# A hybrid block on one core: state-free products in one go, VectorE order anchored to matmuls, unscaled attention probabilities and tanh gates

## The chip, the cores and the metric

The kernel runs on one core of a Trainium2 chip. A core has five engines that work in parallel, each through its own instructions in order: TensorE (PE, matmuls and transposes; its weight loads are shown as PEld), VectorE (DVE), ScalarE (ACT), GpSimd (POOL) and SyncE (SP), which only issues DMAs. DMAs can also be issued from the queues of ACT and POOL. The metric is the device time of one execution in microseconds (us), the median over runs.

## The reference

One block of a network on 1024 tokens of width 1024, in fp32. An input norm is followed by a projection into three groups: q, k, v and a forget gate for 8 attention heads of 64; r, k, v and small low-rank paths for 8 recurrent heads of 64 (RWKV-7); and 2 x 1024 gate columns. Attention adds the running sum of the log forget gate to the logits, is causal, and ends in a softmax:

```python
logits = einsum('bhqd,bhkd->bhqk', q[:, :, q0:q1], k[:, :, :q1]) * scale
logits = logits + cum[:, :, q0:q1, None] - cum[:, :, None, :q1]
probs = softmax(where(causal, logits, -inf))
outs.append(einsum('bhqk,bhkd->bhqd', probs, v[:, :, :q1]))
```

The recurrence carries a 64x64 state per head over the tokens:

```python
sa = einsum('bhvk,bhk->bhv', state, a_t)
state = state * w_t[:, :, None, :] + sa[..., None] * b_t[:, :, None, :] + v_t[..., None] * k_t[:, :, None, :]
y_t = einsum('bhvk,bhk->bhv', state, r_t)
```

Both outputs are projected, multiplied by sigmoid of their gate columns, added and projected again (`wo`). A second norm, a gated feed-forward part of width 2816 with a convolution of three tokens, and a last norm end the block.

## The kernel before

Large products are done to nearly fp32 accuracy by splitting each operand into a rounded part and a remainder (`hi` and `lo`, written by a cast and a subtraction) and adding three matmuls. The stages in time are: the front (modulation, first norm) to 148 us; the recurrence, woven with the projections, to 655; attention, woven with the late gates, to 870; the branch projections `br` to 957, `wo` to 1056; the feed-forward up part (X, W, Y) to 1485 and its down part (D) to the end.

PE's order is written out by hand, by `Weave`. It keeps a clock `now`, advanced by a cost for each matmul emitted. Chains (generators) yield the time after which they want to go on; between them `fill` emits *filler* matmuls from a queue of projections (`qk`, `ps_rkv`, `v`, `gt`, later `rk_ps`). In the recurrence only PE is ordered so; a scheduler orders DVE, ACT, POOL and SP by itself. In attention DVE and ACT follow the written order too.

*Recurrence.* Eight units (4 head pairs `p` times 2 halves `hf` of the tokens) each have 8 chunks of 64 tokens. `pre` makes a unit's operands: the scan `cum` (L741), the vectors `ar`, `bk` and others on DVE, the products `p` masked into E (L789), which go through DRAM (`sm`) to the layout M; DVE inverts M in 31 steps of two operations (L809, L811), and the result E32 goes through DRAM (`se`) into TT (L814 to L823). `main` runs behind it, for the unit before: two transposes X<-TT on DVE (L866), then the products xi, zi, uw, mz, and the loop over chunks. For each chunk `fixed` emits the state-free products, two matmuls into `sp` and two into `yp`; two matmuls with the state S0 add to `sp`; DVE makes the next state S by a scaling (L929); two more matmuls with S0 add to `yp`; then 1.15 us of filler.

*Attention.* For each head `load_head` loads q and k (stA 128 rows, stB 68 rows) and v (vh) from POOL's queue. `s_chain` makes the logits `lg` of one block of 128 queries, `softmax` takes the maximum (L1075, DVE), the exp with its sum (L1079, ACT), the reciprocal (L1084) and scales P by it (L1085, DVE). `t_chain` transposes P on PE into `tp`, `halve` splits it (th on ACT, L1112; tl on DVE, L1115), `a_chain` multiplies with v into `ov`, and `collect` adds the two halves of `ov` into `o` (L1146 ACT, L1148 DVE); POOL splits a finished `o` into fx (L1155, L1156). Between these, `late_gate` emits 14 gate halves into the single PSUM tile `rk_ps`; `gate_out` evacuates one by five ACT operations (L1179 to L1187) and an addition on DVE (L1185) and stores it to d_gate. The weights of the late gates are split on POOL (L255, L259). Norms take ln and exp of a sum of squares (L287, L288 in `rms_rstd`); the norm behind `wo` is done in two halves of the tokens. ACT's functions come in sets, and a change of set is a row ACT_TABLE_LOAD; `use_ln_exp` (L195 to L199) asks for the set that has both ln and exp, at the start, after the sigmoids and ahead of the last norm.

Of the kernel before, what the change touches and what calls it, by code (L numbers as in the profile page):

```python
# [16 lines left out]
S = 1024  # L17
# [30 lines left out]
class Weave:  # L48
# [67 lines left out]
    def run(self, chains):  # L116

        self.live = [[self.now, 1 + i, g] for i, g in enumerate(chains)]
        while self.live:
            due = min((c for c in self.live if c[0] <= self.now), key=lambda c: (c[1], c[0]), default=None)  # L120
            if due is None:
                self.fill(min(c[0] for c in self.live))
                continue
            wait = next(due[2], None)
            if wait is None:
                self.live.remove(due)
            else:
                due[0] = self.now + max(wait, 0.0)
# [3 lines left out]
def hybrid_block(ctx: ExitStack, tc: tile.TileContext, a, out):  # L132
# [4 lines left out]
    def mm(o, lhsT, rhs, start, stop, more=False):  # L137

        weave.mm_cost(o, lhsT, rhs)
        nc.tensor.matmul(o, lhsT, rhs, start=start, stop=stop, skip_group_check=more)  # L140
# [34 lines left out]
    epsr = cp.tile([128, 3], F32, name="epsr")  # L175
# [28 lines left out]
    d_v = dr.tile([8, 128, 8, 128], F32R, name="d_v")  # L204
    d_orw = dr.tile([4, 128, S], F32, name="d_orw")
# [39 lines left out]
    def load_w(src, name, pool=None, n=1024, scale=None, tags=("whi", "wlo"), bufs=2):  # L245
# [7 lines left out]
        lo = pool.tile([128, n], F32R, tag=tags[1], name=f"lo_{name}", bufs=bufs)  # L253
        if weave.late == 1:
            i = nc.gpsimd.tensor_copy(hi, raw)  # L255
            if "head" in marks:
                tc.add_manual_dep(i.ins, marks["head"].ins.name, NOSYNC)
            for c in range(0, n, 256):
                nc.gpsimd.tensor_tensor(lo[:, c : c + 256], raw[:, c : c + 256], f32(hi[:, c : c + 256]), op=ALU.subtract)  # L259
        else:  # L260
            nc.scalar.copy(hi, raw)  # L261
            for c in range(0, n, NH):
                nc.vector.tensor_tensor(lo[:, c : c + NH], raw[:, c : c + NH], f32(hi[:, c : c + NH]), op=ALU.subtract)  # L263
# [71 lines left out]
    with ExitStack() as es:  # L335
# [388 lines left out]

        def pre(k, p, hf):
# [15 lines left out]
            nc.vector.tensor_tensor_scan(cum, C("reset"), cum, initial=0.0, op0=ALU.mult, op1=ALU.add)  # L741
            el = chunk_tile("el", 1, NCU, CH + 1)
            nc.gpsimd.memset(el[:, :, 0:1], 1.0)
            nc.scalar.activation(el[:, :, 1:], c3(cum), AF.Exp, scale=-DEC)
            en = tmp("en")
            nc.scalar.activation(en, cum, AF.Exp, scale=DEC)
# [5 lines left out]
            yield from head_sums(ssq, ksq, parts[:, 0, :], parts[:, 1, :])  # L752
            rn = tmp("ksq")
# [48 lines left out]
            ready = weave.now + (46000 if k == 0 else 38500)  # L802
            E32 = chunk_tile("E32", 1, 8, 32)
            nc.gpsimd.tensor_copy(E32, C("einit").rearrange("p (j t) -> p j t", t=32))
            t32 = tmp("t32", 256)
            for s in range(31):
                J, W = s // 4 + 1, 31 - s
                tv = t32[:, 0 : J * W].rearrange("p (j w) -> p j w", w=W)
                tt(tv, E32[:, 0:J, s : s + 1].to_broadcast([128, J, W]),  # L809
                   M32[:, s : s + 1, s + 1 : 32].to_broadcast([128, J, W]), op=ALU.mult)  # L810
                tt(E32[:, 0:J, s + 1 : 32], E32[:, 0:J, s + 1 : 32], tv, op=ALU.add)  # L811
            se = scr.tile([2, NCU, 2, 32, 32], F32, tag="se", name=f"se{n}")
            for g in range(4):
                nc.sync.dma_start(  # L814
                    se.rearrange("h c b (j g) t -> (h c b) g j t", g=4)[:, g, :, :],
                    E32[g * 32 : g * 32 + 32, :, :])
# [1178 lines left out]
```

## Time and profile before

| | us |
|---|---|
| median of 3 runs (lowest, highest) | 1701.3 (1697.85, 1704.96) |
| profiled execution: its time; span from first to last instruction | 1704.73; 1703.0 |
| recurrence, 148 to 655: PE busy, DVE busy, ACT busy | 489.3, 340.4, 216.2 of 507 |
| attention, 655 to 870: PE busy, DVE busy, ACT busy, POOL busy | 202.5, 165.5, 141.8, 52.4 of 215 |
| rest, 870 to 1485: PE busy | 614.9 of 615 |

A row of the profile names the line, the engine, the operation and its output and inputs by the program's names; "x4" counts equal instructions in a row, and brackets give idle time before it and what ended it. PE has the smallest idle time in every stage, and the table gives where it has any.

### The profile page before, as it was taken

Reading aid. Unit: us, or ns where it says so; the run is one execution under the profiler, and the core shown is the slowest. Engines: PE = TensorE matmul, PEld = TensorE weight load, DVE = VectorE, ACT = ScalarE, POOL = GpSimd, SP = SyncE. Lnnn points to the kernel's source line nnn. Section 1 sums busy time; section 2 is a strip of 40 time slices with the busy share of each in tenths; the row PEclk is TensorE's granted clock in tenths of the full one; section 3 lists DMA queues with packets and bytes.
Section 4 is the critical chain, followed back from the end, with each engine's and each line's share of the span. In section 5 each row is a group of like instructions: output and inputs, shape, how many; then the busy total and the mean of one; then the engine's idle time right before and its main releaser. Section 6 shows DMA issues by size and latency. Waiting matters only on the chain.

```text
span 1703.0 us, 26042 instructions
## 1 busy us (share of the span) xinstructions
PE 1638.0 (96%) x9772; PEld 1342.0 (79%) x9772; DVE 1220.8 (72%) x2390; ACT 808.6 (47%) x1482; POOL 143.4 (8%) x175
## 2 busy tenths in 40 slices
PE   5899999998999998999999999999999999999998
PEld 4767777786877776988878888888888888888886
DVE  5776787778676633888877634897777777787677
ACT  5453334333444554766642323654444444454455
POOL 0010101110111003123112000000000000000000
PEclk8899999999999999999999999999999999999999
DMA  8487743533342326433277611132333233484463
GB/s 328 139 314 205 192 125 97 136 106 106 91 115 75 91 81 151 141 110 107 76 265 268 246 62 63 50 105 94 123 107 103 93 117 101 163 284 153 125 215 112
DMA packets 120974, 239.85 MB, mean 141 GB/s; under 512 B 39888, under 2 KB 48336, under 8 KB 120848
## 3 DMA queue, kind: packets, MB, share of 16 engines
q1 hardware_dynamic: 112896, 220.94, 40.0%
q0 software_dynamic: 7952, 17.25, 3.8%
q8 instruction: 77, 1.26, 0.3%
q14 instruction: 49, 0.40, 0.1%
HBM read 172.59 MB, written 65.54 MB: 140 GB/s over the span
## 4 chain that ended last, share of the span: by engine, by line
PE 79%; DVE 9%; DMA 6%; ACT 2%; issue 2%; SPq 1%; DVEq 0%; ACTq 0%
PE X L140 13%; PE D L140 12%; PE Y L140 6%; PE wo L140 5%; PE br L140 5%; PE gt L140 5%; PE rk_ps L140 4%; PE qk L140 4%; PE ps_rkv L140 4%; PE W L140 3%; PE lg L140 2%; PE v L140 2%; PE ov L140 2%; PE sp L140 2%; PE tp L144 2%
## 5 line engine op out<-in xcount | busy, mean ns | idle before, releaser
L140 PE MATMUL D<-op,op 128*128 128x512 f32 x924 | 209.8, 390 | 0.0
L140 PEld LDWEIGHTS D<-op,op 128*128 128x128 f32 x924 | 173.5, 188 | 36.2 <-DVE op L1258 0.3
L140 PE MATMUL X<-T_m,S 128*128 128x512 f32 x440 | 107.3, 390 | 0.2
L140 PEld LDWEIGHTS X<-T_m,S 128*128 128x128 f32 x440 | 82.5, 188 | 18.2 <-ACT x L1534 0.6
L1257 ACT CAST op<-g 128x512 fp32r<-128x512 f32 x77 | 47.8, 621 | 74.1 <-PE D L140 48.0
L1258 DVE TENSOR_TENSOR op<-g,op 128x512 fp32r<-128x512 f32 x77 | 53.0, 689 | 41.7 <-ACT op L1257 41.7
L1494 DVE SCALAR_TENSOR_TENSOR c<-ab,vec,c 128x512 f32<-128x512 f32 x88 | 65.9, 750 | 19.5 <-ACT c L1497 17.9
L809 DVE TENSOR_TENSOR t<-E,M 128x60 f32<-128x60 f32 (+24 forms) x248 | 57.9, 233 | 30.2 <-DMA M<-sm 24.9
L1458 DVE TENSOR_TENSOR S<-ur,S 128x512 fp32r<-128x512 f32 x66 | 45.5, 691 | 35.6 <-ACT S L1454 35.5
L263 DVE TENSOR_TENSOR lo_in<-raw_in,hi_in 128x512 fp32r<-128x512 f32 x84 | 56.5, 707 | 16.1 <-PE gt L140 13.9
L1454 ACT CAST S<-ur 128x512 fp32r<-128x512 f32 x66 | 41.0, 622 | 55.6 <-DVE ur L1447 30.6
L1458 DVE TENSOR_TENSOR A<-ur,A 128x512 fp32r<-128x512 f32 x64 | 44.1, 688 | 30.9 <-ACT A L1454 30.7
L261 ACT CAST hi_in<-raw_in 128x1024 fp32r<-128x1024 f32 x42 | 44.0, 1049 | 44.3 <-PE ps_rkv L140 16.0
L140 PE MATMUL Y<-T_h,A 128*128 128x512 f32 x264 | 63.5, 390 | 0.0
L140 PE MATMUL Y<-T_h,S 128*128 128x512 f32 x264 | 63.3, 390 | 0.0
L140 PE MATMUL X<-B_b,A 128*128 128x512 f32 x252 | 60.8, 391 | 0.0
L140 PE MATMUL W<-B_f,A 128*128 128x512 f32 x252 | 60.6, 390 | 0.0
L1079 ACT ACTIVATE P<-lg,nm 128x896 f32<-128x896 f32 (+3 forms) x64 | 47.4, 743 | 22.8 <-DVE nm L1075 22.6
L811 DVE TENSOR_TENSOR E<-E,t 128x60 f32<-128x60 f32 (+24 forms) x248 | 53.8, 217 | 5.8
L140 PEld LDWEIGHTS Y<-T_h,A 128*128 128x128 f32 x264 | 49.6, 188 | 10.3
L140 PEld LDWEIGHTS Y<-T_h,S 128*128 128x128 f32 x264 | 49.6, 188 | 10.3
L1454 ACT CAST A<-ur 128x512 fp32r<-128x512 f32 x64 | 39.9, 623 | 34.2 <-PE X L140 31.5
(473 smaller groups left out, 4169.0 us busy)
## 6 DMA issues: line engine op xcount, KB each, us to landing
raw_in<-in_w_in SPq DMA_DIRECT2D x50, 512.0 KB, 3.7
wm<-in_w_mod SPq DMA_DIRECT2D x48, 512.0 KB, 7.0
ur<-in_w_up SPq DMA_DIRECT2D x44, 512.0 KB, 4.2
g<-d_g SPq DMA_DIRECT2D x35, 512.0 KB, 4.0
d_g<-gs SPq DMA_DIRECT2D x44, 256.0 KB, 2.0
d_g<-c SPq DMA_DIRECT2D x33, 256.0 KB, 4.4
d_st<-qh SPq DMA_DIRECT2D x64, 128.0 KB, 2.5
d_gate<-gs SPq DMA_DIRECT2D x32, 256.0 KB, 2.9
```

The lines of the kernel that those rows point to most:

```text
L140: nc.tensor.matmul(o, lhsT, rhs, start=start, stop=stop, skip_group_check=more)
L144: nc.tensor.transpose(o, i, eye)
L261: nc.scalar.copy(hi, raw)
L263: nc.vector.tensor_tensor(lo[:, c : c + NH], raw[:, c : c + NH], f32(hi[:, c : c + NH]), op=ALU.subtract)
L809: tt(tv, E32[:, 0:J, s : s + 1].to_broadcast([128, J, W]), M32[:, s : s + 1, s + 1 : 32].to_broadcast([128, J, W]), op=ALU.mult)
L811: tt(E32[:, 0:J, s + 1 : 32], E32[:, 0:J, s + 1 : 32], tv, op=ALU.add)
L1079: nc.scalar.activation(e[:, 0:n], lg[:, 0:n], AF.Exp, bias=nm[:, 0:1], accum_out=nm[:, 1:2])
L1257: nc.scalar.copy(hi, src)
L1258: tt(lo, src, f32(hi), op=ALU.subtract)
L1454: nc.scalar.copy(hi, src)
L1458: tt(lo, src, f32(hi), op=ALU.subtract)
L1494: stt(c, ab[:, x + hf * NH : x + hf * NH + NH], V("conv_w", 22 * x + i), c, op0=ALU.mult, op1=ALU.add)
```

## The change

*Recurrence.* The state-free products of all eight chunks are emitted in one go ahead of the chunk loop. Three DVE operations are *anchored*: a dependency without a wait puts them in the scheduler's order behind the matmul emitted last. These are the scan (now behind the ssq product), the first step of the inversion (spawned 8.5 us of the clock behind the `p` products) and the X transposes (1.5 us ahead of xi). `Weave.run` holds back the chain of `pre` when a step of `main` is due within 2.6 us.

*Attention.* For heads 0 to 6 P isn't scaled. The sums of four query blocks are collected, inverted by one reciprocal, transposed by PE (four rows), copied by ACT, stored to DRAM (d_rs) and loaded back, broadcast over 64 rows; both DMAs are issued from ACT's queue, and the load waits for the store. POOL multiplies the finished `o` with it. Head 7 goes as before. The first head is loaded by five DMAs of its own (`load_first`), so that the two buffers of `load_head` are both free for heads 1 and 2. A late gate is one tanh and one scaling with an offset; its weights are split on ACT and DVE. The table of exp and tanh is loaded by a preload of its own, and the one of ln and exp is asked for again after attention.

```diff
@@ Weave @@
-    def run(self, chains):
+    def run(self, chains, beside=0.0):
...
+        led = False
         while self.live:
             due = min((c for c in self.live if c[0] <= self.now), key=lambda c: (c[1], c[0]), default=None)
-            if due is None:
-                self.fill(min(c[0] for c in self.live))
+            lead = min((c[0] for c in self.live if c[1] < 2), default=None)
+            if due is None or (due[1] > 1 and not led and lead is not None and lead < self.now + beside):
+                self.fill(min(c[0] for c in self.live) if due is None else lead)
+                led = False
                 continue
+            led = beside > 0 and (led or due[1] < 2)
...
-        nc.tensor.matmul(o, lhsT, rhs, start=start, stop=stop, skip_group_check=more)
+        weave.last = nc.tensor.matmul(o, lhsT, rhs, start=start, stop=stop, skip_group_check=more)
+
+    def behind(i):
+        tc.add_manual_dep(i.ins, weave.last.ins.name, NOSYNC)
...
@@ load_w @@
+        nc.scalar.copy(hi, raw)
         if weave.late == 1:
-            i = nc.gpsimd.tensor_copy(hi, raw)
...
-            for c in range(0, n, 256):
-                nc.gpsimd.tensor_tensor(lo[:, c : c + 256], raw[:, c : c + 256], f32(hi[:, c : c + 256]), op=ALU.subtract)
-        else:
-            nc.scalar.copy(hi, raw)
-            for c in range(0, n, NH):
-                nc.vector.tensor_tensor(lo[:, c : c + NH], raw[:, c : c + NH], f32(hi[:, c : c + NH]), op=ALU.subtract)
+            weave.use("ACT", weave.now, 900)
+            weave.use("DVE", weave.now, 1200)
+        for c in range(0, n, NH):
+            nc.vector.tensor_tensor(lo[:, c : c + NH], raw[:, c : c + NH], f32(hi[:, c : c + NH]), op=ALU.subtract)
...
@@ the recurrence: inverse() holds lines 804 to 823 of before @@
+        def inverse(n, M32, TT, chunk_tile, tmp):
...
+                i = tt(tv, E32[:, 0:J, s : s + 1].to_broadcast([128, J, W]),
+                   M32[:, s : s + 1, s + 1 : 32].to_broadcast([128, J, W]), op=ALU.mult)
+                if s == 0:
+                    behind(i)
...
@@ pre @@
-            nc.vector.tensor_tensor_scan(cum, C("reset"), cum, initial=0.0, op0=ALU.mult, op1=ALU.add)
...
             yield from head_sums(ssq, ksq, parts[:, 0, :], parts[:, 1, :])
+            behind(nc.vector.tensor_tensor_scan(cum, C("reset"), cum, initial=0.0, op0=ALU.mult, op1=ALU.add))
...
-            ready = weave.now + (46000 if k == 0 else 38500)
...
+            ready = weave.now + (47500 if k == 0 else 38500)
             TT = chunk_tile("TT", 2, NCU, CH)
+            weave.spawn(inverse(n, M32, TT, chunk_tile, tmp), 8500)
...
@@ main @@
+            yield max(0, o["ready"] - weave.now - 1500)
             for h in range(2):
-                nc.vector.transpose(X[B0[h], :, :], TT[B0[h], :, 0:32])
-            yield max(0, o["ready"] - weave.now)
+                behind(nc.vector.transpose(X[B0[h], :, :], TT[B0[h], :, 0:32]))
+            yield 1500
...
-            def fixed(c):
-
+            for c in range(NCU):
                 alone = hf == 0 and c == 0
...
-            fixed(0)
             yield 2400
...
                     yield 1150
-                    fixed(c + 1)
...
-        weave.run([main_chain(), pre_chain()])
+        weave.run([main_chain(), pre_chain()], beside=2600.0)
@@ attention @@
+    def load_first():
+
+        parts = [d_st[0, 0], d_st[0, 1], d_st[0, 2, 0:68, :], d_st[0, 3, 0:68, :], d_v[0].rearrange("p a x -> p (a x)")]
+        tiles = [fxp.tile([128, S], F32R, tag=f"h{t}", name=f"first{t}") for t in (3, 7, 2, 6, 5)]
+        for t, x in zip(tiles, parts):
+            marks["head"] = nc.gpsimd.dma_start(t[0 : x.shape[0], :], x)
+        heads[0] = *tiles[0:4], tiles[4].rearrange("p (a x) -> p a x", x=128)
...
-    load_head(0)
+    load_first()
...
-            yield 10500
+            yield 3500
...
-            nc.scalar.activation(e[:, 0:n], lg[:, 0:n], AF.Exp, bias=nm[:, 0:1], accum_out=nm[:, 1:2])
+            p, hf = h // 2, i // 4
+            if (h, hf) not in sums:
+                sums[h, hf] = at.tile([128, 8], F32, tag="sums", name=f"sums{h}_{hf}", bufs=4), []
+            sm, done = sums[h, hf]
+            total = nm[:, 1:2] if h == 7 else sm[:, i % 4 : i % 4 + 1]
+            nc.scalar.activation(e[:, 0:n], lg[:, 0:n], AF.Exp, bias=nm[:, 0:1], accum_out=total)
...
-            nc.vector.reciprocal(nm[:, 2:3], nm[:, 1:2])
-            ts(e[:, 0:n], e[:, 0:n], nm[:, 2:3], None, op0=ALU.mult)
+            if h == 7:
...
+                ts(e[:, 0:n], e[:, 0:n], nm[:, 2:3], None, op0=ALU.mult)
...
+            if h < 7 and len(done) == 4:
+                yield t + 140 - weave.now
+                nc.vector.reciprocal(sm[:, 4:8], sm[:, 0:4])
+                inverse[h, hf] = weave.use("DVE", weave.now, 160) + 210, sm
+
+        def spread(h, hf, tp):
+            p = h // 2
+            rt = at.tile([4, 128], F32, tag="rt", name=f"rt{h}_{hf}", bufs=1)
+            nc.scalar.copy(rt, tp[0:4, 384:512])
+            t = weave.use("ACT", weave.now, 200)
+            nc.scalar.dma_start(d_rs[h, hf * NH : hf * NH + NH].rearrange("(i k) -> i k", k=128), rt)
...
+            yield t + 3500 - weave.now
+            nc.scalar.dma_start(norms[p, hf][h % 2 * 64 : h % 2 * 64 + 64, :],
+                                d_rs[h : h + 1, hf * NH : hf * NH + NH].to_broadcast([64, NH]))
+            landed.add((h, hf))
...
+                    last = jj == I and I in (1, 2) and h < 7
+                    if last:
...
+                        transpose(tp[0:4, 384:512], sm[:, 4:8], ident)
...
+            n = len(got)
+            if n == (2 if p == 3 else 4):
+                while (6 if p == 3 else h, hf) not in landed:
+                    yield 100
+                r = slice(0, 64 if p == 3 else 128)
+                for x in (slice(0, 256), slice(256, NH)):
+                    nc.gpsimd.tensor_tensor(o[r, x], o[r, x], norms[p, hf][r, x], op=ALU.mult)
...
-            nc.scalar.activation(g, rk_ps, AF.Abs)
-            nc.scalar.activation(m, rk_ps, AF.Relu, scale=-1.0)
-            weave.hold = weave.use("ACT", weave.now, 960) + 210
-            nc.scalar.activation(g, g, AF.Exp, scale=-1.0)
-            nc.scalar.activation(g, g, AF.Ln, bias=1.0)
...
-            tt(g, g, m, op=ALU.add)
...
-            nc.scalar.activation(g, g, AF.Exp, scale=-1.0)
+            nc.scalar.activation(g, rk_ps, AF.Tanh, scale=0.5)
+            weave.hold = weave.use("ACT", weave.now, 480) + 210
+            nc.scalar.activation(g, g, AF.Identity, scale=0.5, bias=epsr[:, 3:4])
...
+        nc.scalar.preload_act_table_set("exp_and_others")
         weave.run([a_chain(), t_chain(), s_chain()])
         weave.late = 2
         weave.run([drain()])
+    use_ln_exp()
```

Three places in the order. First DVE in the recurrence, where unit (1,1) runs its chunks (S1_1x is the state behind chunk x, made for the matmuls `sp` of the next chunk) while unit (2,0) waits for its transposes X2_0. Before:

```order
L929 TENSOR_SCALAR S1_11_4305<-sp1_1_4237,pcd1_1_2866 128x64
L763 SCALAR_TENSOR_TENSOR kr2_1_4247<-kr2_1_4247,vec_72,al2_1_4159 128x512
L866 STREAM_TRANSPOSE X2_0_4698<-TT2_0_3868 32x256
L764 TENSOR_TENSOR bk2_1_4249<-kr2_1_4247,en2_1_4165 128x8x64
L767 TENSOR_SCALAR al2_1_4159<-al2_1_4159,vec_72,oka_88 128x512
L866 STREAM_TRANSPOSE X2_0_4698<-TT2_0_3868 32x256
L929 TENSOR_SCALAR S1_12_4321<-sp1_1_4237,pcd1_1_2866 128x64
L768 TENSOR_TENSOR al2_1_4159<-al2_1_4159,k21_3355 128x512
L769 TENSOR_TENSOR bk2_1_4249<-al2_1_4159,en2_1_4165 128x8x64
L773 SCALAR_TENSOR_TENSOR ksq2_1_4261<-r21_3354,vec_72,al2_1_4159 128x512
L929 TENSOR_SCALAR S1_13_4337<-sp1_1_4237,pcd1_1_2866 128x64
```

and now:

```order
L939 TENSOR_SCALAR S1_16_4412<-sp1_1_4233,pcd1_1_2913 128x64
L821 TENSOR_TENSOR E2_1_4429<-p1_2_100_4432,cst2_122 128x4x128
L821 TENSOR_TENSOR E2_1_4429<-p1_2_110_4433,cst2_122 128x4x128
L268 TENSOR_TENSOR lo_v11_4379<-raw_v11_4376,hi_v11_4378 128x512 x2
L363 SCALAR_TENSOR_TENSOR v30_4071<-ps_rkv110_4384,omu_81,sh_rkv110_4453 128x512
L359 COPY sh_rkv31_5562<-pv3r_4314 128x1
L957 SCALAR_TENSOR_TENSOR y1_1_4426<-mu1_1_4428,y1_1_4426 128x512
L821 TENSOR_TENSOR E2_1_4429<-p1_2_104_4493,cst2_122 128x4x128
L821 TENSOR_TENSOR E2_1_4429<-p1_2_114_4494,cst2_122 128x4x128
L990 TENSOR_TENSOR vs1_0_4507<-v1_0_4465,vs1_0_4507 128x4x64
L848 COPY QA2_1_4430<-at2_1_4548 64x4x64 x4
L879 STREAM_TRANSPOSE X2_0_4603<-TT2_0_3839 32x256 x2
```

The transposes of the next unit stood between the second and the third state of a unit; now they stand behind its last state and its first normalisation step (y1_1).

Second, ACT in attention, about the end of head 0 (P is an exp, th a copy of transposed P, o an evacuation of `ov`, gs a gate, rt the sums, R their broadcast). Before:

```order
L1079 ACTIVATE P1_6_7207,nm1_6_7169<-lg1_6_7155,nm1_6_7169 128x896
L1112 CAST th0_22_7229<-tp0_22_7223 128x384
L1079 ACTIVATE P1_7_7242,nm1_7_7219<-lg1_7_7199,nm1_7_7219 128x1024
L1112 CAST th0_10_7265<-tp0_10_7256 128x512
L1146 COPY o01_7146<-ov_6889 64x256
L1112 CAST th0_11_7279<-tp0_11_7267 128x384
L1179 ACTIVATE gs10_1_7281<-rk_ps_6890 128x512
L1180 ACTIVATE gm10_1_7282<-rk_ps_6890 128x512
L1182 ACTIVATE gs10_1_7281<-gs10_1_7281 128x512
L1183 ACTIVATE gs10_1_7281<-gs10_1_7281 128x512
L1079 ACTIVATE P1_0_7308,nm1_0_7297<-lg1_0_7273,nm1_0_7297 128x128
```

and now:

```order
L1100 ACTIVATE P1_6_7146,sums1_1_7147<-lg1_6_7110,nm1_6_7127 128x896
L1119 COPY rt0_1_7149<-tp0_22_7118 4x128
L1121 DMA d_rs_97<-rt0_1_7149 4x128
L1195 COPY o01_7079<-ov_6895 64x256
L1100 ACTIVATE P1_7_7180,sums1_1_7147<-lg1_7_7138,nm1_7_7164 128x1024
L1159 CAST th0_10_7187<-tp0_10_7174 128x512
L1236 ACTIVATE gs9_1_7190<-rk_ps_6896 128x512
L1238 ACTIVATE gs9_1_7190<-gs9_1_7190,epsr_76 128x512
L1159 CAST th0_11_7198<-tp0_11_7182 128x384
L1100 ACTIVATE P1_0_7213,sums1_0_7214<-lg1_0_7194,nm1_0_7203 128x128
L263 CAST hi_in37_7220<-raw_in37_7218 128x1024
L1125 DMA R01_7152<-d_rs_97 64x512
```

The gate has two operations instead of five, the cast hi_in has come from POOL, and the store d_rs and the load R are issued with eight operations between them.

Third, ACT at the second half of the norm behind `wo` (the squares of the last rows, then ln and exp of the sums ssq2). Before:

```order
L1393 ACTIVATE wo6_0_10599,ssq2_10020<-h_sb6_10315 128x512
L1393 ACTIVATE wo6_1_10603,ssq2_10020<-h_sb6_10315 128x512
L1393 ACTIVATE wo7_0_10658,ssq2_10020<-h_sb7_10317 128x512
L1393 ACTIVATE wo7_1_10662,ssq2_10020<-h_sb7_10317 128x512
L287 ACTIVATE ssq2_10020<-ssq2_10020,epsr_76 128x4
L288 ACTIVATE ssq2_10020<-ssq2_10020 128x4
```

and now:

```order
L1448 ACTIVATE wo6_0_10543,ssq2_9964<-h_sb6_10259 128x512
L1448 ACTIVATE wo6_1_10547,ssq2_9964<-h_sb6_10259 128x512
L1448 ACTIVATE wo7_0_10602,ssq2_9964<-h_sb7_10261 128x512
L1448 ACTIVATE wo7_1_10606,ssq2_9964<-h_sb7_10261 128x512
L292 ACT_TABLE_LOAD
L292 ACTIVATE ssq2_9964<-ssq2_9964,epsr_76 128x4
L293 ACT_TABLE_LOAD
L293 ACTIVATE ssq2_9964<-ssq2_9964 128x4
```

Ln and exp each have a table load of their own; the preload written after attention stands at the start of ACT's order, in row 2.

112 lines of the change are left out of this document (61 added, 51 removed).

## The prediction

> **What bounds the kernel now.** I read the page's head and its chain of work first, then the busy time by stage.
>
> ```profile
> PE 1638.0 (96%) x9772; PEld 1342.0 (79%) x9772; DVE 1220.8 (72%) x2390; ACT 808.6 (47%) x1482; POOL 143.4 (8%) x175
> ...
> PE 79%; DVE 9%; DMA 6%; ACT 2%; issue 2%; SPq 1%; DVEq 0%; ACTq 0%
> ```
>
> ```profile
> 148.00:655.00 507.00, 489.29 (x4362) 390.23 (x4361) 340.44 (x968) 216.22 (x378) 58.92 (x83) 0.99 0.41 114
> 655.00:870.00 215.00, 202.46 (x1215) 176.48 (x1214) 165.48 (x324) 141.79 (x320) 52.42 (x64) 0.97 0.42 117
> ```
>
> TensorE is the bound: 96% of the span, and 79% of the chain that ended last. No matmul product is taken out by the change, so it can gain only where PE stands still. The second view (columns: window, its length, then busy us and count of PE, PEld, DVE, ACT, POOL, then clock) has the two stages that the change touches: the recurrence (148 to 655), where PE is idle for 507.00 - 489.29 = 17.7 us, and the attention (655 to 870), with 12.5 us. That is the whole prize, but for what a stall leaves behind. The waits of PE say whose these are, first in the recurrence, then in the attention (to 872):
>
> ```profile
> PE sp L140 <- DVE S L929: 8.6, 5, 3.5
> PE xi L140 <- DVE X L866: 3.0, 2, 1.6
> PE p L140 <- DVE bk L769: 2.0, 1, 2.0
> PE ps_rkv L140 <- DVE k L358: 1.6, 1, 1.6
> PE at L144 <- DVE E L789: 1.0, 1, 1.0
> ```
>
> ```profile
> PE rk_ps L140 <- ACT gm L1180: 4.7, 2, 4.5
> PE ov L140 <- DVE o L1148: 3.2, 2, 2.2
> PE br L140 <- ACT hi_br L1231: 2.1, 1, 2.1
> ```
>
> The largest of the recurrence is PE waiting for the state S. VectorE's timeline at one of its five waits shows why S is late, and PE's what follows:
>
> ```profile
> 421.72 0.43 DVE L866 STREAM_TRANSPOSE X<-TT 32x256 f32<-32x256 f32 x1 [3.80 <-DMA TT<-se]
> ...
> 423.68 0.28 DVE L929 TENSOR_SCALAR S<-sp,pcd 128x64 f32<-128x64 f32 x1
> ```
>
> ```profile
> 424.02 0.47 PE L140 MATMUL sp<-UV,E 128*64 128x64 f32 x4 [3.46 <-DVE S L929]
> ...
> 425.25 2.44 PE L140 MATMUL ps_rkv<-u_hi,lo_in 128*128 128x512 f32 x5
> ```
>
> S itself takes 0.28 us. It was queued behind an X transpose of the *next* unit, which waited 3.80 us for a DMA. And after the 3.46 us gap five matmuls take 2.44 us, where five take about 1.15 at the usual 0.23 each: a tail of 1.3 us. Of the five waits for S two are long (this one and one at 531 us), so the recurrence loses 17.7 + 2 x 1.3 = 20.3 us. In the attention, ScalarE and VectorE rows:
>
> ```profile
> 665.92 0.60 ACT L1179 ACTIVATE gs<-rk_ps 128x512 f32<-128x512 f32 x1 [5.46 <-DMA d_gate<-gs]
> ```
>
> ```profile
> 660.58 1.98 PE L140 MATMUL rk_ps<-u_hi,lo_in 128*128 128x512 f32 x8
> 667.06 3.78 PE L140 MATMUL rk_ps<-u_hi,hi_in 128*128 128x512 f32 x8 [4.51 <-ACT gm L1180]
> 670.64 3.22 PE L140 MATMUL rk_ps<-u_lo,hi_in 128*128 128x512 f32 x8
> ```
>
> ```profile
> 737.69 3.66 DVE L1085 TENSOR_SCALAR P<-P,nm 128x384 f32<-128x384 f32 x1
> ...
> 741.92 0.49 DVE L1085 TENSOR_SCALAR P<-P,nm 128x512 f32<-128x512 f32 x1
> ```
>
> ```profile
> 738.34 2.79 POOL L259 TENSOR_TENSOR lo_in<-raw_in,hi_in 128x256 fp32r<-128x256 f32 x4
> ```
>
> A gate evacuation waited for the store of an earlier gate (4.51 us on PE, then a tail of (3.78 - 1.98) + (3.22 - 1.98) = 3.0). A scaling of P took 3.66 us where a larger one takes 0.49, and it spans the whole of GpSimd's four subtractions; the `ov` matmul behind it waited 2.2, with a tail that I estimate at 2.3 (between the 1.3 and 3.0 above). So the attention loses 12.5 + 5.3 = 17.8 us.
>
> **The change, part by part.** *Recurrence order.* In the changed order the X transposes of a unit stand behind the last S of the unit before (the order shown above), the scan behind the ssq product, the inversion 8.5 us of PE's time later. Summed over the recurrence, VectorE's longest waits are
>
> ```profile
> DVE S L929 <- PE sp L140: 27.4, 24, 2.8
> DVE t L809 <- DMA M<-sm: 24.9, 7, 6.7
> DVE X L866 <- DMA TT<-se: 23.3, 12, 4.9
> ```
>
> The last two, those of the inversion and of the X transposes, are 48 us of head-of-line blocking. Of this, and of the scan's wait for its input, PE felt 8.6 (sp), 1.6 (ps_rkv, k behind the scan) and 1.0 (at). These 11.2 and the tails of 2.6 go: 13.8. The waits of unit 0 stay (xi 3.0, p 2.0), since nothing runs before it that its order could be put behind. But the anchors are no free good: with the products in one go a step of the state loop loses 0.38 us of PE work that used to lie between S and its use:
>
> ```profile
> 629.74 0.34 PE L140 MATMUL sp<-UV,E 128*64 128x64 f32 x4
> ...
> 630.12 0.33 PE L140 MATMUL sp<-S,Mt 64*64 64x64 f32 x4
> ```
>
> From 629.74 to 630.12 are the state-free products of a chunk, behind them those with the state. VectorE's rows between two S are unchanged in sum, so about ten of the sixty steps, those with over 2.2 us of VectorE rows between them by the changed order, now make PE wait. Bounds: 0 and the whole 0.38 in each of sixty steps, 23; I take 0.4 in ten, 4 us, as most steps hold under 2 us of such rows. The products themselves are the same matmuls; batching them saves between 0 and 0.1 for each of 56 groups (their starts are already close), I take 2. Recurrence: 13.8 - 4 + 2 = 12 us, bounds 0 and 25.
>
> *Attention.* Three of five gate operations, the lo_in subtractions on GpSimd and the P scaling of seven heads leave: 42 operations of ScalarE, 56 scalings and 14 additions of VectorE. Neither is the bound, so by themselves they are worth what PE waited for them: 4.5 + 3.0 (the first gate), 2.2 + 2.3 (the 3.66 us scaling, which can't recur without the GpSimd subtractions), 2.1 for hi_br (in the changed order 42 gate matmuls, moved and not removed, cover that end) and half of the remaining 3.7, so 16. New on PE: 14 transposes of four rows at about 0.11 (the 64-row groups above are 0.1 each), 1.5. New in front: the first head's logits come 35 matmuls (8 us at 0.23) behind the last `va`, where 54 stand before, and their second operands are 68-row loads, the third and fourth of five, with three heads loading at once instead of two. The 128-row load of 1 MB and, in the second row, the 68-row one of 544 KB take, from issue to landing:
>
> ```profile
> stA<-d_st POOLq DMA_DIRECT2D x7, 1024.0 KB, 5.9
> ```
>
> ```profile
> DMA to landing us min/median/max: 11.5/12.8/18.6
> ```
>
> In the changed kernel the latter comes in two halves, issued behind GpSimd's last operation of the recurrence and the 128-row loads, so about at the last `va`, 8 us before PE asks for them. In half of 11.5 they land in time, in the whole 12.8 they land 5 us late; I take 1.5. *The Trainium skill, "DMA: Bandwidth & Descriptors", section "Why a DMA increments its semaphore by 16 and not by 1", says that a transfer is spread over the largest number up to 16 that divides its rows, so 68 rows use 4 engines. The trace agrees in so far as this load, of half the bytes, takes twice as long as the 128-row one; by the rule two halves on separate engines would land in time, and this term would be 0.*
>
> *ScalarE's queue.* 14 times a store of the sums and a broadcasting load that waits for it are issued from ScalarE, with 5 to 9 operations (3 to 5 us at 0.6) between them; ScalarE is in order, so exp and the tp copies stand behind that wait. The nearest row is the gates' store:
>
> ```profile
> DMA to landing us min/median/max: 2.0/2.8/7.9
> ```
>
> At the median it costs nothing, at the longest 3 to 5 us each. I take three late by 0.5 us beyond PE's buffers, 1.5 us; bounds 0 and 14 x 4 = 56. Attention: 16 - 1.5 - 1.5 - 1.5 = 11.5, bounds 17 and a loss.
>
> *Table loads.* After attention the set with both ln and exp isn't reloaded in place (the load is hoisted to the start, so ScalarE's order shows), and each half of the norm behind `wo` gets two loads. Of the second half, ScalarE's exp, PE's rows and a load:
>
> ```profile
> 1061.10 0.21 ACT L288 ACTIVATE ssq<-ssq 128x4 f32<-128x4 f32 x1
> ```
>
> ```profile
> 1059.19 2.96 PE L140 MATMUL W<-B_f,A 128*128 128x512 f32 x12
> 1061.98 3.73 PE L140 MATMUL tr<-dg,h_sb 128*128 128x128 f32 x32
> ```
>
> ```profile
> L197 ACT ACT_TABLE_LOAD x3 | 3.8, 1283 | 0.1
> ```
>
> This half is on PE's path: `tr` starts 0.7 us after the exp, with no PE work in front to cover it. Two loads make it 2 x 1.28 = 2.6 later, and a gap over 2.2 us has a tail, 1.3 by the recurrence's: 3.9. The first half has the wo products of the other half between its exp and its `tr` as cover and costs nothing; without them it would be the same 3.9. Two more loads at the start I count as 0.4, since the squares there wait for x's loads. *The Trainium skill, "ScalarE: Activation LUTs", section "What ACT_TABLE_LOAD costs", gives a drain of 1.38 us on top of each load: the norm would then cost 5.3 and its tail. The row above has 0.1 us of idle time before three loads together, which leaves no room for a drain ahead of them; I stay with 2.6.*
>
> Sum: 12 + 11.5 - 3.9 - 0.4 = 19 us.
>
> **How this stands to the median.** The profiled execution took 1704.73 (span 1703.0, 1.7 around it); the three runs are 1697.85, 1701.3 and 1704.96, so it is 3.4 above the median, and one of its random waits may be in my sum. I take the 19 from the median: 1701.3 - 19 = 1682.
>
> **Rivals.** *S becomes the bound.* The anchors trade DMA waits for waits behind VectorE's own rows: a step is 0.38 shorter on PE, VectorE's is not. For it: VectorE is 67% busy there, more around the steps. Against it: 24 of 60 S waited for PE, not PE for S. At 0.25 in each of 60 steps, 15 us instead of 4: 1693. *First head late.* The halves of the 68-row loads land like a whole one in company (18.6 was the longest), PE waits 5 with a tail of 3: 1689, and with the rival above 1700. *Everything hidden*: no new S waits (+4), no wait at the first head or for the sums (+3), the batch at its 5.6 (+3.6), all other attention waits gone (+2), no tail at the norm (+1.3): 1668. *Slower*: ScalarE's queue. If the stores of the sums land like the slowest gate store (7.9) behind 4.5 us of operations, exp and th stand 3.4 us each time; less a buffer of about 1 that is 2.4 x 14 = 34 us, and the time 1682 + 34 = 1716. It decides from 19/14 = 1.4 us of PE time per round trip on; for it speaks that the DMA engines are 42% busy in this stage, against it that such a store holds 2 KB and the gate's 256. *The change doesn't do what it says*: "anchored" order adds no wait of its own, and the batch adds no work, so a null result would have to be the S rival and the first head together.
>
> **How the numbers follow.** Forecast 1682, 0.52 (own range 1673 to 1692); everything hidden, 0.17; one or both of the first two rivals so far that it lands within 0.5% of 1701.3 (1692.8 to 1709.8), 0.19; slower beyond it, 0.12. Half a percent is about what the runs can tell, as three runs of one kernel spread by 0.4%. So faster 0.69, same 0.19, slower 0.12. The range reaches from 1662 (all 38.1 us of the two stages and half of the batch's 5.6, less 1.5 of transposes) to 1704, to take in most of the small-gain cases.
>
> **What would show it.** X transposes without a DMA wait between S rows; PE's wait for S below 5 us; no 3.66 us scaling; `lg` of head 0 waiting under 2 us; ScalarE's waits for the d_rs store under 5 us in sum; two table loads right before the ln and exp of the norm's second half and a PE gap of 2.6 there. I am wrong if PE's wait for S grows, or if ScalarE's waits for d_rs pass 20 us.

## The result and the profile after

The changed kernel takes 1678.97 us (median of 4 runs, 1677.63 to 1679.31), the kernel before 1699.57 in the same session (4 runs, 1696.57 to 1704.96): a ratio of 0.987, 95% interval 0.985 to 0.989, so 20.6 us less. The forecast was 1682. The sum came out, but its two large terms did not, and that the total is so close is luck: the recurrence gained twice what was forecast, and attention nothing. The page's head and the chain of the changed kernel:

```profile
PE 1622.2 (97%) x9786; PEld 1331.6 (79%) x9786; DVE 1189.7 (71%) x2291; ACT 807.5 (48%) x1467; POOL 137.8 (8%) x169
...
PE 81%; DVE 8%; ACT 4%; DMA 3%; issue 2%; SPq 0%; POOL 0%; ACTq 0%; DVEq 0%; POOLq 0%
```

Its busy time by stage; the recurrence now ends at 622 and attention with the gates behind it at 842:

```profile
148.00:622.00 474.00, 468.91 (x4345) 378.48 (x4344) 345.08 (x964) 213.73 (x374) 60.53 (x77) 1.00 0.43 121
622.00:842.00 220.00, 204.73 (x1236) 177.04 (x1235) 129.22 (x227) 133.12 (x300) 44.59 (x60) 0.98 0.47 130
```

PE's idle time fell from 17.7 to 5.1 us in the recurrence, and rose from 12.5 to 15.3 in attention. Stage by stage, from the first row of each in the two traces (1703.0 and 1677.5 us long; the profiled execution of before took 1704.7, over its median, so they differ by 25.5 and not by 20.6):

| from, to | before | after |
|---|---|---|
| start, first product p | 171.9 | 167.8 |
| first p, last va (recurrence) | 482.3 | 453.9 |
| last va, first br (attention, gates) | 214.7 | 219.8 |
| first br, first X | 187.6 | 187.4 |
| first X, first D (norm's second half in it) | 429.1 | 431.5 |

The granted clock (the share of its full clock at which TensorE was let run) is 0.983 over the trace of before and 0.989 over that after: by an estimate 0.006 of 1700 us, 10 of the 25.5 us between the traces. Before, three stretches of 3.4 us in the recurrence, at 232.9, 424.1 and 533.3 us, each at a wait of PE, ran at about 0.5; after, its clock is 1.00. Seven gate matmuls, 1.6 us, have moved from the second row into the third. The first row isn't the change's: p starts between 165.6 and 171.9 over all the traces of this study, and at 168.4 in a kernel whose front is that of before.

PE's waits in the recurrence after, then in attention and the gates after it:

```profile
PE qk L144 <- DVE v L363: 2.2, 1, 2.2
PE sp L144 <- DVE S L939: 1.5, 3, 0.9
PE zi L144 <- ACT X L886: 0.5, 1, 0.5
```

```profile
PE lg L144 <- ACT P L1100: 4.7, 7, 1.2
PE tp L151 <- DVE tl L1164: 4.7, 2, 3.7
PE rk_ps L144 <- ACT gs L1236: 3.6, 5, 0.9
PE tp L151 <- DVE nm L1106: 0.9, 1, 0.9
PE ov L144 <- DVE tl L1164: 0.7, 1, 0.7
```

Of the rows that the prediction names only a rest of that for S is left in either list. In the recurrence little has come in their place (qk waited 0.9 before); in attention the waits for the exp have grown (0.6 before), those for `tl` at the transposes are new, and a gate is waited for five times shortly in place of once for long. VectorE's rows at the place shown before, unit (1,1), now run without the X transpose between the states:

```profile
403.06 0.28 DVE L939 TENSOR_SCALAR S<-sp,pcd 128x64 f32<-128x64 f32 x1
...
404.51 0.28 DVE L939 TENSOR_SCALAR S<-sp,pcd 128x64 f32<-128x64 f32 x1
...
407.70 0.28 DVE L939 TENSOR_SCALAR S<-sp,pcd 128x64 f32<-128x64 f32 x1 [0.20 <-PE sp L144]
```

The longest of the new waits, on PE, VectorE and ScalarE:

```profile
738.73 1.11 PE L151 MATMUL tp<-cst,P 128*128 128x128 f32 x4 [3.70 <-DVE tl L1164]
```

```profile
736.05 2.02 DVE L268 TENSOR_TENSOR lo_in<-raw_in,hi_in 128x512 fp32r<-128x512 f32 x2 [5.80 <-ACT hi_in L263]
738.00 0.68 DVE L1164 TENSOR_TENSOR tl<-tp,th 128x512 fp32r<-128x512 f32 x1
```

```profile
734.97 1.05 ACT L263 CAST hi_in<-raw_in 128x1024 fp32r<-128x1024 f32 x1
```

The remainder of a gate weight (lo_in), which was GpSimd's, is now written into VectorE's order at the same point as the cast that it needs into ScalarE's: `load_w` charges both engines from one `weave.now` and does not wait for the cast. ScalarE was done with the cast 5.8 us later, and tl, which frees the buffer that the transposes of P need, stood behind it. It is the same kind of block as X behind its DMA, in another place. Five of the six late weights do it, 13.6 us of VectorE in sum.

### The profile page after: what moved, and what is told of

It reads as the page before. It is cut to its first block, busy times and chain, and to the rows that moved or that the text cites. A ratio compares the mean times of both kernels' runs of the same rounds, so it can differ in the third digit from the quotient of the medians.

```text
span 1677.5 us, 26048 instructions
## 1 busy us (share of the span) xinstructions
PE 1622.2 (97%) x9786; PEld 1331.6 (79%) x9786; DVE 1189.7 (71%) x2291; ACT 807.5 (48%) x1467; POOL 137.8 (8%) x169
## 4 chain that ended last, share of the span: by engine, by line
PE 81%; DVE 8%; ACT 4%; DMA 3%; issue 2%; SPq 0%; POOL 0%; ACTq 0%; DVEq 0%; POOLq 0%
PE X L144 13%; PE D L144 12%; PE Y L144 6%; PE gt L144 6%; PE ps_rkv L144 5%; PE br L144 5%; PE wo L144 5%; PE rk_ps L144 3%; PE qk L144 3%; PE W L144 3%; PE v L144 3%; PE ov L144 2%; PE lg L144 2%; PE tp L151 2%; PE low L144 1%
## 5 line engine op out<-in xcount | busy, mean ns | idle before, releaser
L268 DVE TENSOR_TENSOR lo_in<-raw_in,hi_in 128x512 fp32r<-128x512 f32 x96 | 66.4, 729 | 28.0 <-ACT hi_in L263 17.2
L1164 DVE TENSOR_TENSOR tl<-tp,th 128x512 fp32r<-128x512 f32 (+1 forms) x80 | 49.5, 633 | 33.3 <-ACT th L1159 32.7
L263 ACT CAST hi_in<-raw_in 128x1024 fp32r<-128x1024 f32 x48 | 50.2, 1049 | 45.0 <-PE ps_rkv L144 26.6
```

The costliest lines, as they stand in the source:

```text
L1164: tt(tl[:, 0:w], tp[:, 0:w], f32(th[:, 0:w]), op=ALU.subtract)
```

## The experiments

The first question was where the gain sits. Two kernels each have one part of the change.

**Recurrence part alone**: of the diff of the change the hunks of `Weave.run`, `behind`, `inverse`, `pre`, `main` and `beside`, nothing from attention on.

> The recurrence part alone (products in one go, anchors, the held-back chain of pre), attention, gates and table loads as before. Theory of the two traces: nearly the whole gain of the change is here, because PE's waits between the first product p and the first branch product fell in the recurrence from about 26 to 8 us and stayed near 20 in attention; then the time is 1677 to 1680. Rival, the split of the prediction (12 us here, 11.5 in attention, 4 lost on table loads): 1687 to 1689.

1673.5 us (1672.5 to 1674.5) against 1700.2 of before, a ratio of 0.984, interval 0.983 to 0.986. More than the whole gain, and 5.5 us faster than the full change.

**Attention part alone**: everything else, with the recurrence as before.

> The attention part alone (unscaled P, sums through DRAM, first head loaded apart, tanh gates, weight split on ACT and DVE, table loads), recurrence as before. Theory of the traces: it is worth nothing or costs a little, 1698 to 1702, since new waits (tp behind tl, lg behind the exp, rk_ps behind the tanh) stand where the old ones were and the norm pays 2 us. Rival, the split of the prediction: 1691 to 1693.

1710.2 us (1704.9 to 1713.2), a ratio of 1.006, interval 1.004 to 1.008: slower by 10 us, worse than both expectations. On top of the new recurrence the same part costs 5.5 (1678.97 against 1673.49). PE's waits in it are those of the full change, row by row (lg 4.7, tp 4.6, rk_ps 3.6), 15.1 us in all against 12.0 before, so the part trades old waits for as many new ones and a few more; the norm adds 2.3 in its trace. Why it is 10 rather than 5.5 here isn't settled: its profiled execution, at some 1707, was faster than its median, and shows 2 to 3 us.

**The table load in place.**

```diff
-            nc.scalar.activation(g, rk_ps, AF.Tanh, scale=0.5)
+            marks["gate"] = nc.scalar.activation(g, rk_ps, AF.Tanh, scale=0.5)
-    use_ln_exp()
+    use_ln_exp(marks["gate"])
```

> The changed kernel with one edit: the load of the table of ln and exp after attention is ordered behind the last tanh, so that the norm behind wo has no loads of its own. If the two loads are all that holds PE at the norm's second half (a gap of 1.9 us in the trace), the time falls by 2 to 3 us, to 1676 to 1677, and the gap goes. If the gap has another cause (the squares or the diagonal come late), no change, 1679.

1676.2 us (1672.4 to 1679.3): 2.8 less. The changed kernel's norm, ScalarE and then PE, and PE in the experiment:

```profile
1033.00 1.28 ACT L292 ACT_TABLE_LOAD   x1
1034.30 0.30 ACT L292 ACTIVATE ssq<-ssq,epsr 128x4 f32<-128x4 f32 x1
1034.61 1.28 ACT L293 ACT_TABLE_LOAD   x1
1035.91 0.20 ACT L293 ACTIVATE ssq<-ssq 128x4 f32<-128x4 f32 x1
```

```profile
1036.49 3.73 PE L144 MATMUL tr<-dg,h_sb 128*128 128x128 f32 x31 [1.90 <-DVE dg L1416]
```

```profile
1034.74 3.73 PE L144 MATMUL tr<-dg,h_sb 128*128 128x128 f32 x32
```

The gap is gone with the loads. X to D is 429.1 again, against 431.5. The ranges of the times overlap, so the gain rests on these rows.

**The remainders back on GpSimd**, with the same written order:

```diff
-        for c in range(0, n, NH):
-            nc.vector.tensor_tensor(lo[:, c : c + NH], raw[:, c : c + NH], f32(hi[:, c : c + NH]), op=ALU.subtract)
+        for c in range(0, n, 256):
+            nc.gpsimd.tensor_tensor(lo[:, c : c + 256], raw[:, c : c + 256], f32(hi[:, c : c + 256]), op=ALU.subtract)
```

> The changed kernel with one edit: the remainders of the late gate weights are subtracted on GpSimd again (pieces of 256) instead of on VectorE, the rounding stays on ScalarE, the written order is the same. Theory: VectorE's five waits for ScalarE's cast (13.6 us, the longest 5.8) hold up tl and so the transposes; without them PE gains 5 to 8 us, 1671 to 1674. Rival one: the P chain is bound by its own latency and the waits only move, 1678 to 1680. Rival two: GpSimd's subtractions slow VectorE as the 3.66 us row of the kernel before, at least one stall of over 2 us on PE comes back, 1680 to 1684.

1681.7 us (1681.4 to 1686.8), and by the time alone the second rival. The trace says otherwise: PE's waits for tl are gone, but GpSimd's scheduler had put the first subtraction ahead of the first head's loads:

```profile
PE lg L144 <- DMA first<-d_st: 9.3, 2, 7.0
PE lg L144 <- ACT P L1103: 5.0, 7, 1.2
PE rk_ps L144 <- ACT gs L1239: 2.7, 4, 0.7
```

```profile
627.31 2.85 POOL L268 TENSOR_TENSOR lo_in<-raw_in,hi_in 128x256 fp32r<-128x256 f32 x4 [7.24 <-PE gt L144]
630.08 2.18 POOL L1036 DMA_DIRECT2D first<-d_st  x4
```

So the edit was repeated with the subtractions ordered behind those loads, and the table load in place:

```diff
+                tc.add_manual_dep(i.ins, marks["head"].ins.name, NOSYNC)
```

> The changed kernel with the table load in place (as e3_norm, 1676.2 us) and the late weights' remainders on GpSimd (as e4_lo_pool), but ordered behind the five loads of the first head, which e4_lo_pool had pushed behind the first remainder (PE waited 10 us for them there). Theory: without VectorE's waits for ScalarE's cast PE's waits for tl (about 6 us with their tail) go: 1669 to 1672. Rival: they only move to the next wait, 1675 to 1678.

1666.2 us (1663.8 to 1672.2), a ratio of 0.980 to before, interval 0.977 to 0.983: 9.9 less than with the table load alone. Its waits in attention:

```profile
PE lg L144 <- ACT P L1104: 5.9, 7, 1.9
PE rk_ps L144 <- ACT gs L1240: 3.6, 5, 0.9
```

The waits for tl, nm and P (6.8 us in the changed kernel, with slower matmuls behind the 3.7 us gap) are gone, those for the exp and the gate stay. From last va to first br it takes 211.4 against 219.8. The theory holds: this move turned the attention part from a gain of some 7 us into a loss. (It also takes the subtractions themselves off VectorE; no run separates that from their place in its order.)

**Which piece of the recurrence.** Each of the next four takes a piece away or adds one alone. Without the batch (products of a chunk emitted between two states, as before):

```diff
-            for c in range(NCU):
+            def fixed(c):
...
+            fixed(0)
             yield 2400
...
                     yield 1150
+                    fixed(c + 1)
```

> The recurrence part alone (as e1_rec, 1673.5 us) with the state-free products of a chunk emitted between two states again, as before; anchors and the held-back chain stay. In the traces the starts of the sp and yp products take 47.8 us before and 38.8 with the batch. Theory: the batch itself is worth 9 us, since a narrow product between two wide ones pays for the change, and the time rises to 1681 to 1684. Rival, as predicted: it is worth 2 us and the rest of the gain is order alone, 1674 to 1677.

1697.3 us (1695.4 to 1700.9): 24 more, far beyond the 9 expected. The starts of the sp and yp products do take 47.1 us again, against 38.8, so 8.3 is the batch. In the traces the stretch from the first p to the first br is 20.8 longer; another 7.0 are PE's waits (25.1 against 18.1), nearly all in attention, which was not edited. Its rows there, and the gate matmuls of the two kernels (first this one, then the recurrence part alone):

```profile
PE rk_ps L144 <- ACT gm L1195: 6.8, 2, 6.6
PE ov L144 <- DVE o L1163: 3.2, 2, 2.2
PE br L144 <- ACT hi_br L1246: 2.1, 1, 2.1
PE rk_ps L144 <- DVE gs L336: 2.0, 1, 2.0
```

```profile
L144 PE MATMUL rk_ps<-u_hi,hi_in 128*128 128x512 f32 x96 | 30.7, 451 | 8.7 <-ACT gm L1195 6.8 <-DVE gs L336 2.0
```

```profile
L144 PE MATMUL rk_ps<-u_hi,hi_in 128*128 128x512 f32 x112 | 34.7, 441 | 5.5 <-ACT gm L1191 5.5
```

Filler is a budget, as I read it: a recurrence that is longer on the planner's clock uses more gate matmuls as filler, here two halves (48 matmuls), and attention has that much less to put between its own chains. No run changes the budget alone. Of the remaining 5 us of the 20.8 the granted clock has most: 0.984 over this trace against 0.986, by an estimate 0.002 of 1694 us, 3.4, and it sits in attention, 0.95 from last va to first br against 0.97.

The batch alone, in the kernel before (the diff above the other way round):

> The kernel before with the batch alone: the state-free products of all chunks in one go, no anchors, no held-back chain, attention as before. Theory: the batch by itself is worth the 9 us that the starts of the sp and yp products show, 1690 to 1693. Rival one: without it the steps are 0.4 us longer and hide VectorE's rows, so the batch alone makes PE wait for S in its place, and the time stays at 1697 to 1702. Rival two, as predicted: 2 us, 1698.

1695.7 us (1692.5 to 1702.8), a ratio of 0.997, interval 0.995 to 0.999: 5 less, between the theory and its rival. sp and yp start within 39.1 us, 8.8 less, and VectorE waits for M and TT as before, so PE still waits for S:

```profile
PE sp L140 <- DVE S L926: 6.5, 5, 2.4
PE xi L140 <- DVE X L866: 3.1, 2, 1.8
```

X transposes without an anchor, written at the start of `main` again, in the recurrence part:

```diff
-            yield max(0, o["ready"] - weave.now - 1500)
             for h in range(2):
-                behind(nc.vector.transpose(X[B0[h], :, :], TT[B0[h], :, 0:32]))
-            yield 1500
+                nc.vector.transpose(X[B0[h], :, :], TT[B0[h], :, 0:32])
+            yield max(0, o["ready"] - weave.now)
```

> The recurrence part alone (as e1_rec, 1673.5 us) with the X transposes written at the start of main again and without an anchor; the scan and the inversion stay anchored. Theory: the transposes that wait for their DMA in front of a state were most of PE's 8.6 us of waits for S and of the tails behind them, so the time rises by 6 to 12, to 1680 to 1686, and VectorE's idle time before X (8.2 us in the changed kernel) grows to over 15. Rival: the held-back chain of pre and the later inversion keep VectorE clear anyway, 1673 to 1676.

1712.3 us (1712.0 to 1712.9): 39 more, slower than before. VectorE's wait is there as expected, but not in front of S:

```profile
DVE X L880 <- DMA TT<-se: 23.6, 9, 6.9
```

```profile
PE xi L144 <- DVE X L880: 11.9, 3, 10.6
PE ov L144 <- DVE o L1158: 6.7, 4, 2.2
PE rk_ps L144 <- ACT gm L1190: 4.2, 2, 3.9
```

S waits are 0.6. X itself now comes too late: the scheduler, with no anchor, put it where one unit's xi waited 10.6 us. 98 more gate matmuls went into the recurrence than before (519 `gt` against 421), four halves fewer were left for attention, and ov waits there. More than half of the loss is a slower clock about these waits: it is 0.973 over this trace against 0.986 in the recurrence part alone, by an estimate 0.013 of 1711 us, 22 of the 39, and 0.50 from 506.6 to 520.2 us, about the 10.6 us wait. So the anchor is needed, though my mechanism for its loss was wrong.

Without the held-back chain of pre:

```diff
-        weave.run([main_chain(), pre_chain()], beside=2600.0)
+        weave.run([main_chain(), pre_chain()], beside=0.0)
```

> The recurrence part alone (as e1_rec, 1673.5 us) without holding back the chain of pre (0 in place of 2600). Theory: the anchors alone order VectorE well enough, and the time stays within 4 us, 1672 to 1678. Rival: without it rows of pre stand between the steps of the state on VectorE and PE waits for S again as in the kernel before, 8 us and a tail, 1681 to 1686.

1687.5 us (1686.2 to 1690.3): 14 more, near the rival's range.

```profile
PE sp L144 <- DVE S L941: 4.2, 5, 1.4
PE qk L144 <- DVE v L365: 3.1, 1, 3.1
```

S waits rise from 1.5 to 4.2, and again two gate halves move out of attention. The rival has the wait right, but the larger share is again the clock, 0.982 over this trace against 0.986, by an estimate 0.004 of 1687 us, 7 of the 14. The pieces are not additive: taken away singly they cost 24, 39 and 14, and together they are worth 27. The anchors of the scan and of the inversion were not taken away singly.

**Pieces of the attention part**, each added to the recurrence part. The tanh gates alone, with the table load in place:

```diff
-            nc.scalar.activation(g, rk_ps, AF.Abs)
-            nc.scalar.activation(m, rk_ps, AF.Relu, scale=-1.0)
...
+            marks["gate"] = nc.scalar.activation(g, rk_ps, AF.Tanh, scale=0.5)
...
+            nc.scalar.activation(g, g, AF.Identity, scale=0.5, bias=epsr[:, 3:4])
...
+    use_ln_exp(marks["gate"])
```

> The recurrence part alone (as e1_rec, 1673.5 us) with one part of the attention change: the late gates by one tanh and one scaling (and the table of ln and exp loaded in place behind them); P scaled as before, weights split on GpSimd, heads loaded as before. In e1_rec's trace PE waits 5.9 us for the gates' evacuation, with 4.8 of tails. Theory: these go with two operations instead of five, 1664 to 1668. Rival: the wait there is for the store of an earlier gate and for the buffer, not for the operations, and it stays: 1671 to 1674.

1669.7 us (1666.1 to 1671.7), 3.8 less than the recurrence alone, between theory and rival. ScalarE, and PE's waits:

```profile
633.21 1.28 ACT L1190 ACT_TABLE_LOAD   x1 [6.79 <-DMA d_gate<-gs]
634.50 0.60 ACT L1190 ACTIVATE gs<-rk_ps 128x512 f32<-128x512 f32 x1
```

```profile
PE rk_ps L144 <- ACT gs L1190: 9.3, 5, 6.7
```

The rival's reason is right: the first gate waits for a store of an earlier gate, however many operations it has. What the gates gain, they gain elsewhere: from start to start, waits included, the ov, tp and lg rows take 8.6 us less, and those of rk_ps 4.7 more.

The first head's own loads and its earlier logits alone:

```diff
-    load_head(0)
+    load_first()
...
-            yield 10500
+            yield 3500
```

> The recurrence part alone (as e1_rec, 1673.5 us) with the first head loaded by its own five DMAs, three heads at once, and its logits 7 us earlier; gates, P and weights as before. Theory: the logits don't wait for the loads (they landed in time in the changed kernel), but the first gate's evacuation still waits for an earlier store under the loads, as with e8_tanh, so the time is 1671 to 1676. Rival one: the 2 us and more that attention starts earlier also end it earlier: 1667 to 1671. Rival two: three heads at once hold the store longer, 1677 to 1682.

1666.1 us (1665.0 to 1670.5), 7.4 less: a little beyond rival one. No gate waits for a store, though each still has its five operations, and the two longest waits from attention to the first br are these:

```profile
PE br L144 <- ACT hi_br L1249: 4.2, 1, 4.2
PE tp L151 <- DVE tl L1133: 1.8, 2, 1.3
```

Last, 0.8 us more hold behind a late gate, in the kernel of 1666.2:

```diff
-            weave.hold = weave.use("ACT", weave.now, 480) + 210
+            weave.hold = weave.use("ACT", weave.now, 480) + 1000
```

> The best so far (e7_lo_norm, 1666.2 us) with 0.8 us more of a hold on the filler matmuls behind each late gate, since PE comes 0.7 to 0.9 us too early to the gate's tile five times (4.5 us). Theory: other attention work takes that time, 1662 to 1665. Rival: no other work is due there, PE waits anyway, and the waits for the exp stay: 1665 to 1668.

1669.3 us (1664.6 to 1673.9), which overlaps 1666.2 (1663.8 to 1672.2): neither a gain nor a loss that can be told. Two kernels tie as the fastest, the recurrence part with the first head's loads (1666.1) and the full change with remainders on GpSimd and the table load in place (1666.2), some 35 us below before and 13 below the change as it was made. No run has the unscaled P alone. As the full change with both repairs is no faster than the first head's loads without it, no run here shows that it gains.

## Why the prediction was right, and where it was wrong

Right in the sum (19 forecast, 20.6 measured), but by luck: its errors offset each other. From the medians of the experiments:

| term | forecast | measured |
|---|---|---|
| recurrence | 12 gained | 26.8 gained (1700.2 to 1673.5) |
| attention | 11.5 gained | 2.7 lost (1673.5 to 1676.2) |
| norm's table loads | 3.9 lost | 2.8 lost (1676.2 to 1679.0) |

The ranges behind the last two rows overlap. The traces agree with them: from last va to first br the recurrence part alone takes 216.9 us and the kernel with the table load in place 220.0, and X to D differs by 2.4.

*Recurrence, right in its mechanism, too small in four terms.* The waits for S, ps_rkv and at went as forecast. "The waits of unit 0 stay (xi 3.0, p 2.0)" failed: neither is in the list after, 5 us. The "tails of 2.6" are three stretches of 3.4 us at about half the clock, 5.1; the third, behind the xi waits, was not counted. "0.4 in ten, 4 us" for new S waits measured 1.5 in three. And the batch, "I take 2", is 8.3 to 9.0 by the starts of its rows, beyond its bound of 5.6. I had read from close starts that nothing is lost there; the rows show what is. State-free products before cost 0.38 us a chunk (629.74 to 630.12 in the prediction's rows). In the batch:

```profile
590.88 0.29 PE L144 MATMUL sp<-UV,E 128*64 128x64 f32 x4
591.00 0.29 PE L144 MATMUL yp<-E,UV 128*64 128x64 f32 x4
591.12 0.29 PE L144 MATMUL sp<-UV,E 128*64 128x64 f32 x4
```

A chunk is 0.24 us (590.88 to 591.12). For 56 chunks that is 8 us. So the terms add up: PE's idle time fell by 12.6 us, where 11.2 less 4 was forecast, the clock gave 5.1 for 2.6 and the batch 8.3 for 2, together 26 of the 26.8.

*Attention, wrong.* "So by themselves they are worth what PE waited for them ... so 16" is the step that failed. The old long waits did go, but the sum had no term for the work that the change put onto VectorE and ScalarE in a written order. I had counted the moved lo_in as relief for GpSimd and never asked what stands behind it on VectorE; it cost about 10 us (1676.2 to 1666.2). The waits for the exp (4.7, 0.6 before) stay, at 4.6 to 5.9, in every version with the whole attention part, and are 0.2 and 0.6 with the tanh or the first head's loads alone; which of the rest makes them no run shows. The short waits for a gate (3.6) come with the tanh: alone it has four, 2.6 us, beside the long one. And the 7.5 us of the first gate were credited to its fewer operations. With two operations it still waited 6.7 us for a store; with five, and the first head's own loads, it did not wait for one. So those loads took the wait away.

*The three small fears in attention were nothing.* The transposes of the sums take 0.4 us in all, by the starts of the rows behind them (1.5 forecast). The first head's logits didn't wait (1.5), as its 68-row halves landed in time. The Trainium skill, "DMA: Bandwidth & Descriptors", section "Why a DMA increments its semaphore by 16 and not by 1", would have given that term as 0, and the trace agrees: two transfers of 68 rows need 4.1 us where one of twice the bytes needed 12.8 at the median before and, at the least, 10.9 in the same trace. How many engines each used no row shows. The first row is of the 128-row pieces.

```profile
first<-d_st POOLq DMA_DIRECT2D x2, 512.0 KB, 4.1
first<-d_st POOLq DMA_DIRECT2D x2, 272.0 KB, 4.1
```

And the rival that was to make it slower, ScalarE stuck behind the sums' store, has no row: the view names no operation of ScalarE that waited for d_rs, and ScalarE's idle time ahead of the 14 issues of the load, which wait for the store, is 1.9 us in all. Only GpSimd waited for the broadcast load, off the path.

```profile
  POOL o L1208: 19.6, 6
```

*Table loads* were right in place and nearly in size: 2 x 1.28, of which PE felt 1.9 and a short tail; the tail of 1.3 was too much, as the clock behind this gap is 1.00. The Trainium skill, "ScalarE: Activation LUTs", section "What ACT_TABLE_LOAD costs", adds a drain of 1.38 us to each; the rows above have the load 0.01 us behind the operation before it and the next operation 0.02 behind the load, so no run here shows the drain.

The rival "S becomes the bound" did not come (1.5 us). That the change would do less than it says came true for half of it, and was priced only as bad luck at the first head.

## What to carry to other kernels

When work moves from an engine that a scheduler orders, and that can wait unharmed, to one with a written order, price what stands behind it there: here subtractions of 0.7 us, ahead of their input for five of six weights, cost 10 us. Order alone, with not one product fewer, was worth more than a stage's worth of saved operations; and where independent matmuls fill the gaps, count them as a budget, because what one stage uses up the next one misses (three runs here fit that, none tests it alone). Read the granted clock beside the waits: by an estimate it is 10 of the 25.5 us between the traces before and after, and 22 of the 39 that the X anchor is worth. Test the parts of a change apart even when its total comes out as forecast.

## What the runs showed that I had not expected

The state-free products of a chunk, two rows of four narrow matmuls in the views, cost 0.38 us when they stand with those of the state between wide matmuls, and 0.24 in a run of their own kind. A load of 68 rows in two halves lands in 4.1 us, as fast as two of 128 rows with nearly twice the bytes. And taking the X anchor away, an ordering without a wait, cost 39 us.
